# Streaming encoder step on one core: one write for the halves of q and k, and the norms of the cached values moved to the last phase

## The chip, the core and the metric

The kernel runs on one core of one Trainium2 chip. The metric is the device time of one execution in microseconds. The engines are named as in the profile: PE (TensorE), DVE (VectorE), ACT (ScalarE), POOL (GpSimd) and SP (SyncE, whose queue issues nearly all DMAs).

## The reference

One layer with two token mixers. A prompt of 2048 rows and a batch of 8 sample streams with 16 new rows each (128 rows in all) go through the same weights; the samples also attend to 512 cached rows each. The model width is 1024; branch a has 4 heads of differential attention (two 64-wide queries and keys, one 128-wide value), branch b 8 heads of stick-breaking attention (64 wide).

```python
h, gate = adaln_modulate(x, c, norm_g, w_ada, b_ada)
qa, ka, va, za, qb, kb, vb, zb, ga, gb = split(h @ w_in)      # qa, ka are turned by rope
# a: p = softmax(q k^T / 8) for both halves; w = p1 - lam p2; oa = w v   (keys up to the row's chunk of 64)
# b: log_a = log_sigmoid(z) + reversed cumsum of log_sigmoid(-z) over later keys; ob = exp(log_a) v
ya = (rms_norm(oa, subln_g) * (1 - lam_init) * silu(za)) @ w_branch_a
yb = (ob * silu(zb)) @ w_branch_b
x = x + gate * (sigmoid(ga) * ya + sigmoid(gb) * yb) @ w_out
y = rms_norm(x, final_g)
```

The outputs are y for prompt and samples, and the new k and v of both branches. Inputs and outputs are fp32.

## The kernel before

**Numbers.** Large products are made on TensorE from fp16 pairs: a tensor x is scaled by a power of two that is worked out from its norm, and split into a high half (x rounded to fp16) and a low half (the rest). `split` (L316) does it with two instructions: the high half by ScalarE, VectorE or POOL, and the low half by a VectorE `scalar_tensor_tensor` (L324) that reads the source and the high half. A norm is taken with `sum_squares` (L299): one ScalarE activation that squares a tile of 128 x 1024 and adds up each row, the sums go through a small matmul with ones (`total`, L236) and `scales` makes the powers of two on VectorE.

**Tiles and units.** The rows are 17 tiles of 128: t = 0 to 15 the prompt, t = 16 (`NT`) the samples. The heads are 8 units u: an even unit is one head of branch a (`kind` 0, with rope), an odd one two heads of branch b (`kind` 1). For each unit every tile is projected (`project`: 512 columns of q, k, v, z by L468 matmuls into the bank `ps_mm`). Its `finish` copies the bank (`pr`, L482), makes the halves of v, k and q (L319 and L324; q in `query`, L502 and L503, with its own form), and stores new keys and values. In even units POOL and VectorE turn q and k by rope first (`rot`), and the halves are made from `rot`; in odd units they are made out of PSUM (`ps_mm`). `transpose_qk` turns the six 128 x 128 blocks on TensorE into `ps_t`.

**Scores.** `scores` makes a tile's scores with L709 and L710 into the banks `ps_s`. In even units follow exponentials and the row maximum (L603). In odd units ScalarE makes sigmoids (L135, `sc_p` and `ps_s`), VectorE scans (L683) and POOL multiplies (L689). ScalarE casts the weights' high half (L617, `sc_n`) and VectorE takes the low half (L620). A DMA on SP's queue transposes the weights (`wt`), and TensorE multiplies them by v (L766 to L771). The projection of a unit runs beside the scores of the one before it.

**Side work in the unit phase.** A list `spare` of 48 small loads and squares (made in `norms()`, one step of the list loads a 512 KB piece into one of the shared buffers `wa`/`wb` and squares the piece of the step before): 16 for the branch and output weights and 32 for the cached values, 4 for each of 4 heads of both caches (sums in `csums`). `norm_at` (L1044) says at which step (u, t) of the scores the list is drawn from. A second list does the same for the cached keys, which are also cut and written back (`keys_at`).

**Last phase.** After the units, every tile goes through the branch products (L1507), the merge and the output product (L1541), tile after tile. Between these pieces stand the samples' attention to the caches: `sample` gives ten steps a unit (`steps`), and a new unit begins every six (`S_PERIOD`). In it the cached values are loaded (`cache`, steps 3 and 4, L839), split by their scale (`values`, steps 6 and 7, L843: ScalarE high, VectorE low), and multiplied (`output_cached`, L884) by transposed weights `dwt`, which a DMA makes of `dsc`. `finish` joins cached and new parts with factors `dsf`. The scales of all cached values come from `csums` in one piece at the start of this phase (`vs`).

**What sets the order.** The code issues pieces in the order of the step lists, with weights of cost that interleave them (the number beside each piece); the engines' own order is then made by the tile scheduler. Each engine takes its instructions in that order. The DMAs of SP's queue start in order too.

Of the kernel before, what the change touches and what calls it, by code (L numbers as in the profile page):

```python
# [26 lines left out]
P = 128  # L27
# [11 lines left out]
STICK = 14  # L39
# [86 lines left out]
def layer_kernel(ctx: ExitStack, tc: tile.TileContext, a: dict):  # L126
# [14 lines left out]
    def kept(x):  # L141
# [12 lines left out]
        "av": a["cache_a_v"][0].rearrange("b (j p) h e -> p (b j) (h e)", p=P),  # L154
        "bk": a["cache_b_k"][0].rearrange("b (j p) h d -> p (b j) (h d)", p=P),
        "bv": a["cache_b_v"][0].rearrange("b (j p) h d -> p (b j) (h d)", p=P),
# [154 lines left out]
    def add_up_all(acc):  # L311
        col = tiny.tile([P, acc.shape[1]], F32, tag="cols", name="cols", bufs=1)
        V.tensor_reduce(out=col, in_=acc, axis=AX.X, op=ALU.add)
        return col

# [114 lines left out]
    csums = con.tile([P, 8, 4], F32, name="csums")  # L430
    osums = con.tile([P, NT + 1, 4], F32, name="osums")
    qs = c01.enter_context(tc.tile_pool(name="qs", bufs=1))
    qbuf = [qs.tile([P, 2, 2, 2, 64], F16, name=f"qbuf{i}") for i in range(2)]
    for qb in qbuf:
        G.memset(qb[:, 1, :, 1, :], 0.0)
# [11 lines left out]
    def project(U, t):  # L447
# [30 lines left out]
        def finish():  # L478
# [13 lines left out]
            qb = qbuf[t % len(qbuf)]  # L492
            k16 = stg.tile([P, 2, 2, 64], F16, tag="k16", name="k16")
# [6 lines left out]
            def query(src, scale):  # L500
                src = src.rearrange("p (c d) -> p c d", d=64)
                S.activation(out=qb[:, 0, :, :, :], in_=src.unsqueeze(2).to_broadcast([P, 2, 2, 64]), func=AF.Identity, scale=scale)  # L502
                V.scalar_tensor_tensor(out=qb[:, 1, :, 0, :], in0=src, scalar=scale, in1=qb[:, 0, :, 0, :], op0=ALU.mult, op1=ALU.subtract)  # L503
            if kind == 0:
                cosT, sinT = box["r"][:, 0:32], box["r"][:, 32:96]
                x4 = pr[:, 0:256].rearrange("p (c f d) -> p c f d", c=4, f=2)
                rot = stg.tile([P, 256], F32, tag="rot", name="rot")
                r2 = stg.tile([P, 256], F32, tag="r2", name="r2", bufs=1)
                G.tensor_tensor(out=rot.rearrange("p (c f d) -> p c f d", c=4, f=2), in0=x4,
                                in1=cosT.unsqueeze(1).unsqueeze(1).to_broadcast([P, 4, 2, 32]), op=ALU.mult)  # L510
                G.tensor_tensor(out=r2.rearrange("p (c f d) -> p c f d", c=4, f=2), in0=x4[:, :, ::-1, :],
                                in1=sinT.rearrange("p (f d) -> p f d", f=2).unsqueeze(1).to_broadcast([P, 4, 2, 32]),
                                op=ALU.mult)
                G.tensor_tensor(out=rot, in0=rot, in1=r2, op=ALU.add)
# [17 lines left out]
            U["q16", t], U["k16", t] = qb, k16  # L532
# [24 lines left out]
    def transpose_qk(U, t):  # L557
        g, i = t // 4, t % 4
        q16, k16 = U.pop(("q16", t)), U.pop(("k16", t))
        pt = bank("t", F16)  # L560
        for c in range(2):
            T.transpose(pt[:, c * P : (c + 1) * P], k16[:, c, :, :].rearrange("p f d -> p (f d)"), id16)
        for f in range(2):
            for c in range(2):
                j = 2 + f * 2 + c
                T.transpose(pt[:, j * P : (j + 1) * P], q16[:, f, c, :, :].rearrange("p r d -> p (r d)"), id16)
# [243 lines left out]
    def sample(U, dec, qpad, cs, vs, parity):  # L810
# [6 lines left out]
        ik, sv, iv = (x[:, i : i + 1] for i in (cache_column(nk, h),) for x in (cs, vs[:, 0:8], vs[:, 8:16]))  # L817

        def fetch():
# [6 lines left out]
            V.tensor_scalar(out=f[:, 2:4], in0=parity, scalar1=iv, scalar2=ls[:, 1:2] if kind == 0 else 2.0 ** -STICK, op0=ALU.mult, op1=ALU.mult)  # L826
# [78 lines left out]
        for i in range(4):  # L905
            steps[i // 2] += [one(keys, i)]
            steps[3 + i // 2] += [one(cache, i)]
            steps[6 + i // 2] += [one(values, i)]
            steps[7 + i // 2] += [one(output_cached, i)]
        steps[2] += [one(queries)]  # L910
        steps[4] += [one(scores_all)]
        steps[9] += [one(finish)]
        return steps

    def norms():
# [3 lines left out]
        srcs += [(caches[name][:, i * 8 : i * 8 + 8, h * P : (h + 1) * P], csums[:, cache_column(name, h), i : i + 1], 1.0)  # L919
                 for name in ("av", "bv") for h in range(4) for i in range(4)]  # L920
# [3 lines left out]
        def one(k):  # L924
# [4 lines left out]
            if k < len(srcs):  # L929
                src, dst, scale = srcs[k]  # L930
                st = free.pop(0)
                load(out=st if len(src.shape) == 2 else st.rearrange("p (j n) -> p j n", n=P), in_=src)
# [111 lines left out]
    def norm_at(u, t):  # L1044
        return u < 7 and t < NT and (t >= 16 if u == 0 else t >= 9 or u == 6)
# [420 lines left out]
    with ExitStack() as c2:  # L1466
# [7 lines left out]
        vs = scales(total(add_up_all(csums), 8), res, "s_c", 8)  # L1474
# [109 lines left out]
        for u in range(8):  # L1584
            for i, pieces in enumerate(sample(units[u], dec, qpad, cs, vs, parity)):
# [60 lines left out]
```

## Time and profile before

| | |
|---|---|
| runs | 2211.17, 2213.17, 2214.8 us (median 2213.17) |
| profiled execution, its own time | 2222.53 us |
| its span | 2220.8 us, mean granted PE clock 0.98 |
| PE busy | 2050.1 us (92%), weight loads 1092.0 us beside it |
| DVE / ACT / POOL busy | 1746.7 (79%) / 1607.0 (72%) / 716.0 (32%) us |
| SP's DMA queue | 446.96 MB, 82.5% of 16 engines |
| units | scores of unit 0 from 132 us, of unit 7 to 1735 us; last phase from about 1755 us |

The span is what the trace covers; the execution's own time is 1.7 us longer. A row of a group has the busy time, the mean of one instruction in ns, and the idle time of the engine just before them with what ended most of it. A row of waits reads "waiting op and line <- the one it waited for: total us, count, the longest". Idle time of an engine counts only where the end of the program waits for it.

### The profile page before, as it was taken

To read this page: it belongs to the slowest core of one execution; us is meant where nothing else is said; L and a number is where in the kernel's file an instruction comes from. 1 tells how busy PE (TensorE), PEld (TensorE's weight loads), DVE (VectorE), ACT (ScalarE), POOL (GpSimd) and SP (SyncE) were. 2 spreads that over 40 slices of the span, in tenths; PEclk is the share of its full clock that TensorE was granted. 3 is DMA by queue.
4 is the path that set the end of the run, shared out by engine and by line. 5 is a ranking of instruction groups with operands and counts; after the bars stand their busy time and mean duration, and the time that the engine had idled before them with its cause. 6 is when DMAs were issued, how large, how long until landed. Compare 5 with 4: busy or idle time off the path is not lost. (4 is left out here: it accounts for less than half of the span.)

```text
span 2220.8 us, 41264 instructions
## 1 busy us (share of the span) xinstructions
PE 2050.1 (92%) x14504; PEld 1092.0 (49%) x14504; DVE 1746.7 (79%) x3787; ACT 1607.0 (72%) x3216; POOL 716.0 (32%) x620
## 2 busy tenths in 40 slices
PE   3899999999999999999989998999898798999997
PEld 1545555555555455555555554555454344444443
DVE  5668868789887788988778888787689778778863
ACT  3978677788877687978677788876588556666631
POOL 0433024356310444742034356301345322112210
PEclk9999999999999999999999999999999899999999
DMA  9777669799796989979878899985777899999862
GB/s 333 258 246 188 129 149 220 180 220 205 196 261 159 221 197 207 204 198 226 201 194 211 180 229 212 250 182 127 159 160 171 197 264 215 243 240 233 226 147 67
DMA packets 820817, 449.98 MB, mean 203 GB/s; under 512 B 551962, under 2 KB 759114, under 8 KB 820096
## 3 DMA queue, kind: packets, MB, share of 16 engines
q1 hardware_dynamic: 819660, 446.96, 82.5%
q8 instruction: 113, 1.85, 0.3%
q14 instruction: 96, 0.79, 0.1%
q10 hardware_dynamic: 948, 0.39, 0.1%
HBM read 229.87 MB, written 86.02 MB: 142 GB/s over the span
## 5 line engine op out<-in xcount | busy, mean ns | idle before, releaser
L689 POOL TENSOR_TENSOR sc_p<-sc_p,sc_n 128x127 f32<-128x127 f32 (+7 forms) x192 | 311.9, 1628 | 668.7 <-DVE sc_n L683 510.6
L468 PEld LDWEIGHTS <-hs 128*128 128x128 f16 x3120 | 294.0, 99 | 324.4 <-issue 13.7
L468 PE MATMUL ps_mm<-wa,hs 128*128 128x512 f16 x1590 | 393.4, 383 | 8.2 <-DMA hs<-hT_d 6.4
L468 PE MATMUL ps_mm<-wb,hs 128*128 128x512 f16 x1530 | 379.4, 381 | 0.0
L683 DVE TENSOR_TENSOR_SCAN sc_n<-ps_s,sc_n,zero_t 128x512 f32<-128x512 f32 x192 | 245.4, 1278 | 34.4 <-ACT ps_s L135 29.3
L544 PE MATMUL ps_t<-wa,hs 128*128 128x512 f16 x1020 | 244.4, 382 | 3.3 <-DVE qst L577 2.2
L709 PE MATMUL ps_s<-k,qst 128*128 128x512 f16 (+3 forms) x640 | 222.9, 349 | 26.2 <-DVE sc_n L683 21.1
L544 PEld LDWEIGHTS <-hs 128*128 128x128 f16 x1632 | 155.3, 99 | 186.2 <-DVE qst L577 6.2
L620 DVE TENSOR_TENSOR sc_n<-sc_p,sc_n 128x128 f16<-128x128 f32 (+7 forms) x192 | 213.3, 1113 | 37.2 <-ACT sc_n L617 36.6
L135 ACT ACTIVATE sc_p<-ps_s,usc 128x512 f32<-128x512 f32 (+3 forms) x320 | 203.7, 637 | 38.5 <-PE ps_s L710 27.0
L710 PE MATMUL ps_s<-k,qst 128*128 128x512 f16 (+3 forms) x640 | 223.3, 350 | 0.0
L617 ACT CAST sc_n<-sc_p 128x128 f16<-128x128 f32 (+7 forms) x192 | 155.2, 809 | 59.6 <-POOL sc_p L689 58.9
L135 ACT ACTIVATE ps_s<-ps_s,usc 128x512 f32<-128x512 f32 (+3 forms) x320 | 196.0, 612 | 0.0
L544 PE MATMUL ps_t<-wb,hs 128*128 128x512 f16 x612 | 152.1, 383 | 6.7 <-DMA hs<-hT_d 3.3
L1541 PE MATMUL ps_o<-wo,wb 128*128 128x512 f16 x672 | 153.1, 383 | 1.8 <-ACT wb L1315 1.8
L770 PE MATMUL ps_o<-v,wt 128*128 128x128 f16 x1088 | 135.6, 224 | 19.0 <-DMA wt<-sc_n 18.9
L603 DVE TENSOR_SCALAR_CACHE_REDUCE sc_p<-ps_s,usc 128x512 f32<-128x512 f32 (+3 forms) x160 | 106.1, 664 | 30.5 <-PE ps_s L710 18.6
L1546 POOL TENSOR_TENSOR x<-m,x 128x512 f32<-128x512 f32 x32 | 47.1, 1472 | 254.8 <-DVE m L1544 192.3
L771 PE MATMUL ps_o<-v,wt 128*128 128x64 f16 x1088 | 127.3, 196 | 0.0
L683 DVE TENSOR_TENSOR_SCAN sc_n<-ps_s,zero_t 128x128 f32<-128x128 f32 (+3 forms) x128 | 104.1, 814 | 28.1 <-ACT ps_s L135 28.1
L770 PEld LDWEIGHTS <-wt 128*128 128x128 f16 x1088 | 101.4, 100 | 47.4 <-DMA wt<-sc_n 21.7
L1507 PEld LDWEIGHTS <-wa 128*128 128x128 f16 x816 | 77.5, 98 | 92.1 <-issue 6.0
(380 smaller groups left out, 4528.6 us busy)
## 6 DMA issues: line engine op xcount, KB each, us to landing
hs<-hT_d SPq DMA_DIRECT2D x132, 512.0 KB, 5.0
g_d<-gt SPq DMA_DIRECT2D x68, 256.0 KB, 3.4
out_dram<-pr SPq DMA_DIRECT2D x204, 64.0 KB, 3.7
o_d<-o SPq DMA_DIRECT2D x136, 64.0 KB, 2.4
wa<-g_d SPq DMA_DIRECT2D x17, 512.0 KB, 6.8
wb<-g_d SPq DMA_DIRECT2D x17, 512.0 KB, 4.9
hs<-o_d SPq DMA_DIRECT2D x17, 512.0 KB, 4.1
wide<-in_w_ada_dram SPq DMA_DIRECT2D x8, 1024.0 KB, 12.6
```

What stands on the lines that cost most here:

```text
L135: i = S.activation(**kw)
L468: T.matmul(box["p"], box["h"][:, hi, k, :], U["w"][k][:, wi, :], start=(n == 0), stop=(n == 3 * KT - 1))
L544: x = T.matmul(box["g"][:, 0:gw], box["h"][:, hi, k, :], U["wg"][k // per][:, k % per, wi, :], start=(j == 0), stop=(j == 3 * KT - 1))
L617: x = S.copy(out=hi, in_=src)
L620: V.tensor_tensor(out=lo, in0=src, in1=hi, op=ALU.subtract)
L683: V.tensor_tensor_scan(out=dst[:, lo : lo + n][:, ::-1], data0=src[:, 0:n][:, ::-1], data1=zero_t[:, 0:1].to_broadcast([P, n]), initial=fi ...
L689: G.tensor_tensor(out=p[:, 0:m], in0=p[:, 0:m], in1=n[:, 1 : m + 1], op=ALU.mult)
L709: T.matmul(p[:, 0:n], qst[:, c, :], kk[:, c, 0:n], start=True, stop=False)
L710: T.matmul(p[:, 0:n], qst[:, 2 + c, :], kk[:, c, 0:n], start=False, stop=not diag)
L770: T.matmul(po[:, c * P : (c + 1) * P], wt[:, wj, :], vt[:, c, :, :], start=first, stop=False)
L771: T.matmul(po[:, c * P : c * P + 64], wt[:, nb + wj, :], vt[:, c, 0, :], start=False, stop=last)
L1541: T.matmul(po, st["y"][:, yi * 8 + k, :], wo[j * 4 + k // 2][:, wi, k % 2, :], start=(n == 0), stop=(n == 3 * KT - 1))
```

## The change

It has two parts. **Halves:** q and k of a tile get one buffer `qkbuf` of four blocks (q, q, k, k) of 64 columns, each as (high, low, high). One ScalarE instruction writes both high copies of all four blocks (512 elements out, 256 in), and one VectorE instruction the four low halves (256 elements). Before there were two of each: ScalarE 256 and 128 elements, VectorE 128 and 128. The transposed blocks take (high, low) or (low, high) as they lie; what was a zero block beside q's low half is now q's high half there, and the memset of the zeros is gone. That is 136 instructions fewer on ScalarE and 136 on VectorE.

**Cached values:** `norms()` no longer reads them: 32 loads of 512 KB and 32 squares leave the unit phase. `norm_at` draws the list, now 17 pieces long, in units 2, 4 and 6 alone. In the last phase `square` takes the norm of the piece that the sample's own load has brought (steps 4 and 5, one step behind the load), and `value_scale` adds it up at the front of step 6: a reduction, a small matmul into a bank `ps_s`, five small VectorE instructions and the factors in `dsf`. The one piece that made all scales at the phase's start is gone.

```diff
+    qkbuf = [qs.tile([P, 4, 3, 64], F16, name=f"qkbuf{i}") for i in range(2)]
-    for qb in qbuf:
-        G.memset(qb[:, 1, :, 1, :], 0.0)
...
-            def query(src, scale):
-                src = src.rearrange("p (c d) -> p c d", d=64)
-                S.activation(out=qb[:, 0, :, :, :], in_=src.unsqueeze(2).to_broadcast([P, 2, 2, 64]), func=AF.Identity, scale=scale)
-                V.scalar_tensor_tensor(out=qb[:, 1, :, 0, :], in0=src, scalar=scale, in1=qb[:, 0, :, 0, :], op0=ALU.mult, op1=ALU.subtract)
+            def queries_keys(src, scale):
+                src = src.rearrange("p (b d) -> p b d", d=64)
+                S.activation(out=qk[:, :, 0:3:2, :], in_=src.unsqueeze(2).to_broadcast([P, 4, 2, 64]), func=AF.Identity, scale=scale)
+                V.scalar_tensor_tensor(out=qk[:, :, 1, :], in0=src, scalar=scale, in1=qk[:, :, 0, :], op0=ALU.mult, op1=ALU.subtract)
...
-                query(rot[:, 0:128], s)
-                halves(k16, rot[:, 128:256], s)
+                queries_keys(rot, s)
...
-                halves(k16, p[:, 128:256], s2)
-                query(p[:, 0:128], s2)
+                queries_keys(p[:, 0:256], s2)
...
+        for j, (b, r) in enumerate(((2, 0), (3, 0), (0, 0), (1, 0), (0, 1), (1, 1))):
+            T.transpose(pt[:, j * P : (j + 1) * P], qk[:, b, r : r + 2, :].rearrange("p r d -> p (r d)"), id16)
...
+        def square(j):
+            if j == 0:
+                box["acc"] = dec.tile([P, 4], F32, tag="dacc", name="dacc", bufs=2)
+            sum_squares(box["vc", j].rearrange("p b n -> p (b n)"), 1024, box["acc"][:, j : j + 1])
+
+        def value_scale():
+            box["sv"] = x = scales(total(add_up(box.pop("acc"), 4), 1, "s"), dec, "dsv")
+            V.tensor_scalar(out=box["f"][:, 2:4], in0=parity, scalar1=x[:, 1:2], scalar2=ls[:, 1:2] if kind == 0 else 2.0 ** -STICK, op0=ALU.mult, op1=ALU.mult)
...
+            steps[4 + i // 2] += [(0.3, lambda i=i: square(i))]
...
+        steps[6].insert(0, (0.3, value_scale))
...
-        srcs += [(caches[name][:, i * 8 : i * 8 + 8, h * P : (h + 1) * P], csums[:, cache_column(name, h), i : i + 1], 1.0)
-                 for name in ("av", "bv") for h in range(4) for i in range(4)]
...
     def norm_at(u, t):
-        return u < 7 and t < NT and (t >= 16 if u == 0 else t >= 9 or u == 6)
+        return u in (2, 4) and 12 <= t < NT or u == 6 and 9 <= t < NT
...
-        vs = scales(total(add_up_all(csums), 8), res, "s_c", 8)
```

The first place is the end of unit 3 on ScalarE, where the projection of unit 4 has begun beside the last scores of unit 3 (`sc_p` and `ps_s` are sigmoids of those, `csums` a square of cached values). Before:

```order
L617 CAST sc_n<-sc_p 128x1024
L502 ACTIVATE qbuf_213<-rot,sq_11249 128x256
L319 ACTIVATE k_11480<-rot,sq_11249 128x2x64
L482 ACTIVATE pr<-ps_mm,usc_11240 128x512
L319 ACTIVATE v<-ps_mm,usc_11240 128x2x64
L135 ACTIVATE sc_p<-ps_s,usc_8227 128x512
L135 ACTIVATE ps_s<-ps_s,usc_8227 128x512
L299 ACTIVATE junk,csums<-wb_1426 128x1024
L135 ACTIVATE sc_p<-ps_s,usc_8227 128x384
L135 ACTIVATE ps_s<-ps_s,usc_8227 128x384
```

And at the same place after the change (line numbers are those of the changed file, 7 to 16 lower):

```order
L601 CAST sc_n<-sc_p 128x1024
L492 ACTIVATE qkbuf_212<-rot,sq_11006 128x4x2x64
L135 ACTIVATE sc_p<-ps_s,usc_8044 128x512
L135 ACTIVATE ps_s<-ps_s,usc_8044 128x512
L472 ACTIVATE pr<-ps_mm,usc_10997 128x512
L312 ACTIVATE v<-ps_mm,usc_10997 128x2x64
L135 ACTIVATE sc_p<-ps_s,usc_8044 128x384
L135 ACTIVATE ps_s<-ps_s,usc_8044 128x384
```

Two instructions for q and k became one, the square between two pairs of sigmoids is gone, and the first pair stands ahead of the next tile's `pr` and `v`.

The second place is ScalarE in the last phase, at the samples' unit 1 (`dsc` and `ps_t`, `ps_s` are its sigmoids, the cast of `dsc` 128 x 640 is what the DMA to `dwt` waits for; `hs`, `wa`, `wb` belong to the branch products). Before:

```order
L135 ACTIVATE dsc<-ps_s,dsf 128x512
L135 ACTIVATE ps_s<-ps_s,dsf 128x512
L135 ACTIVATE hs_181<-hs_181 128x512
L135 ACTIVATE wa_171<-wa_171 128x1024
L135 ACTIVATE wb_1426<-wb_1426 128x1024
L1315 COPY wa_169<-ps_s 128x1024
L1513 CAST wb_1424<-wa_172 128x512
L617 CAST dsc<-dsc 128x640 x2
```

And after (`dacc` takes the squares of the cached values `dc`):

```order
L135 ACTIVATE dsc<-ps_s,dsf 128x512
L135 ACTIVATE ps_s<-ps_s,dsf 128x512
L297 ACTIVATE junk,dacc<-dc 128x1024
L601 CAST dsc<-dsc 128x640
L297 ACTIVATE junk,dacc<-dc 128x1024
L1505 CAST wb_1400<-wa_176 128x512
L601 CAST dsc<-dsc 128x640
```

A square stands ahead of each of the two casts of the weights.

The third place is VectorE in the last phase, at the samples' unit 0 (`nm` to `dsc` is its softmax, `wa` and `wb` the branch products). Before:

```order
L637 TENSOR_REDUCE nm<-mx 128x2
L1509 SCALAR_TENSOR_TENSOR wa_171<-ps_mm,fuy,wa_171 128x512
L651 RECIPROCAL r<-l 128x2
L652 SCALAR_TENSOR_TENSOR r<-l,r,nlam 128x1
L653 TENSOR_TENSOR r<-r,ls_i 128x1
L658 SCALAR_TENSOR_TENSOR dsc<-dsc,r 128x640
```

And after (`col` is the reduction whose sum the small matmul takes, `sc_q` to `dsv` are the scales):

```order
L306 TENSOR_REDUCE col<-dacc 128x1
...
L642 SCALAR_TENSOR_TENSOR dsc<-dsc,r 128x640
L242 TENSOR_SCALAR sc_q<-ps_s 128x1
L244 TENSOR_SCALAR sc_f<-sc_q 128x1
L246 TENSOR_SCALAR sc_e<-sc_f 128x1
L247 TENSOR_SCALAR sc_e<-sc_f 128x1
L249 TENSOR_SCALAR dsv<-sc_e 128x2
L831 TENSOR_SCALAR dsf<-parity,dsv,ls_i 128x2
```

The sum and its scales, which stood once at the phase's start, now stand in each unit, the reduction ahead of the softmax and the scales behind it.

More of the change, by code (lines that the diff above doesn't have):

```diff
@@ L309, in add_up @@
         return col
[L311 to L314, printed above, removed]
     def split(hi, lo, src, s, on=None):
@@ L429, in layer_kernel @@
     cexp = con.tile([P, 8, 4], I32, name="cexp")
-    csums = con.tile([P, 8, 4], F32, name="csums")
     osums = con.tile([P, NT + 1, 4], F32, name="osums")
     qs = c01.enter_context(tc.tile_pool(name="qs", bufs=1))
-    qbuf = [qs.tile([P, 2, 2, 2, 64], F16, name=f"qbuf{i}") for i in range(2)]
-    for qb in qbuf:
-        G.memset(qb[:, 1, :, 1, :], 0.0)
+    qkbuf = [qs.tile([P, 4, 3, 64], F16, name=f"qkbuf{i}") for i in range(2)]
     silu_z = {}
@@ L490, in finish @@
                 S.activation(out=rings[t % len(rings)], in_=p[:, 384:512], func=AF.Identity, scale=sc[:, 1:2])
-            qb = qbuf[t % len(qbuf)]
-            k16 = stg.tile([P, 2, 2, 64], F16, tag="k16", name="k16")
+            qk = qkbuf[t % len(qkbuf)]
             vt = kvp.tile([P, 2, 2, 64], F16, tag="v", name="v", bufs=V_BUFS)
@@ L531, in finish @@
                 load(out=s_d[U["u"]][:, 6:8, :], in_=vt.rearrange("p c f d -> p c (f d)"))
[L532 removed]
+            U["qk", t] = qk
         g0, gw = GATES[U["u"]]
@@ L558, in transpose_qk @@
         g, i = t // 4, t % 4
-        q16, k16 = U.pop(("q16", t)), U.pop(("k16", t))
+        qk = U.pop(("qk", t))
         pt = bank("t", F16)
[L561 to L566, printed above, removed]
+        for j, (b, r) in enumerate(((2, 0), (3, 0), (0, 0), (1, 0), (0, 1), (1, 1))):
+            T.transpose(pt[:, j * P : (j + 1) * P], qk[:, b, r : r + 2, :].rearrange("p r d -> p (r d)"), id16)
         if t == NT:
@@ L808, in cache_column, with sample @@
         return "ab".index(name[0]) * 4 + h
-    def sample(U, dec, qpad, cs, vs, parity):
+    def sample(U, dec, qpad, cs, parity):
         kind, h, t, sc, sq = U["kind"], U["h"], NT, U["sc"], U["sq"]
@@ L816, in sample @@
         box = {}
-        ik, sv, iv = (x[:, i : i + 1] for i in (cache_column(nk, h),) for x in (cs, vs[:, 0:8], vs[:, 8:16]))
+        ik = cs[:, cache_column(nk, h) : cache_column(nk, h) + 1]
         def fetch():
@@ L931, in one @@
                 st = free.pop(0)
-                load(out=st if len(src.shape) == 2 else st.rearrange("p (j n) -> p j n", n=P), in_=src)
+                load(out=st, in_=src)
                 loaded.append((st, dst, scale))
@@ L1584, in layer_kernel @@
         for u in range(8):
-            for i, pieces in enumerate(sample(units[u], dec, qpad, cs, vs, parity)):
+            for i, pieces in enumerate(sample(units[u], dec, qpad, cs, parity)):
                 if S_PERIOD * u + i == len(lane):
```

4 lines of the change are left out of this document (1 added, 3 removed).

## Prediction, as it was put on record before the changed kernel ran

> **What bounds the kernel now.** I read the page first: its head, its first part (busy time) and its second (forty slices). Under the head line come the first part, and then three rows of slices.
>
> ```profile
> span 2220.8 us, 41264 instructions
> PE 2050.1 (92%) x14504; PEld 1092.0 (49%) x14504; DVE 1746.7 (79%) x3787; ACT 1607.0 (72%) x3216; POOL 716.0 (32%) x620
> PE   3899999999999999999989998999898798999997
> DVE  5668868789887788988778888787689778778863
> ACT  3978677788877687978677788876588556666631
> ```
>
> TensorE is busy for 92% of the span and stands at 9 in most slices, so the time is TensorE's own work plus the 171 us (2220.8 less 2050.1) in which it stands idle. The change leaves the large matmuls as they are. It can therefore only move the idle part, and the question for each edit is which of TensorE's waits it shortens or makes.
>
> Next come three windows at the ends of units 1, 3 and 5 and one over most of the sample lane in the last stretch (the columns are busy time and instruction count of PE, PEld, DVE, ACT and POOL, then clock, DMA share and GB/s).
>
> ```profile
> 480.00:550.00 70.00, 63.86 (x519) 36.42 (x517) 66.20 (x115) 65.43 (x136) 48.21 (x42) 0.98 0.95 203
> 888.00:958.00 70.00, 61.92 (x497) 35.17 (x496) 62.64 (x112) 62.94 (x128) 46.07 (x41) 0.96 0.98 203
> 1300.00:1380.00 80.00, 72.54 (x549) 39.76 (x547) 70.08 (x120) 70.86 (x145) 53.39 (x47) 0.94 1.02 206
> 1850.00:2120.00 270.00, 260.23 (x2063) 127.23 (x2064) 218.82 (x501) 171.61 (x241) 54.46 (x38) 0.99 0.89 230
> ```
>
> At the ends of odd units ScalarE (63 of 70 us) and VectorE (63 to 66 of 70) are nearly full and TensorE loses 6 to 8 us each time. In the last stretch ScalarE is busy 64% and TensorE 96%. So the change takes ScalarE work from places where it is scarce and adds it to a place where it has room, but where TensorE has little slack.
>
> **The part taken away from ends of odd units.** In the waits of TensorE, each of the three windows (480 to 530, 888 to 932, 1300 to 1348) gives the same row, the first below. The other rows are the timeline of ScalarE and VectorE at one of these waits.
>
> ```profile
> PE ps_s L709 <- DVE sc_n L683: 4.1, 3, 1.7
> ...
> 516.88 1.04 ACT L617 CAST sc_n<-sc_p 128x1024 f16<-128x1024 f32 x1
> 517.84 1.05 ACT L299 ACTIVATE junk<-wb 128x1024 f16<-128x1024 f32 x1
> 518.79 0.19 ACT L299 ACTIVATION_READ_ACCUMULATOR junk<-wb 128x1 f32 x1
> 518.89 0.67 ACT L135 ACTIVATE sc_p<-ps_s,usc 128x512 f32<-128x512 f32 x1
> ...
> 519.06 1.21 DVE L683 TENSOR_TENSOR_SCAN sc_n<-ps_s,zero_t 128x512 f32<-128x512 f32 x1
> ...
> 520.32 0.38 PE L709 MATMUL ps_s<-k,qst 128*128 128x512 f16 x1 [1.70 <-DVE sc_n L683]
> ```
>
> A score matmul waits 1.70 us for a bank that a scan frees; ScalarE's sigmoids for that unit stand behind a square, which holds the queue from 517.84 to 518.89, 1.05 us. With the change no norm stands in an odd unit. How many do now is counted by the windows of that line alone at the three ends (here the second column is ScalarE's busy time and count).
>
> ```profile
> 480.00:530.00 50.00, 4.68 (x8) 0.97 0.98 199
> 884.00:932.00 48.00, 3.45 (x6) 0.96 1.01 216
> 1297.00:1348.00 51.00, 3.53 (x7) 0.93 1.05 224
> ```
>
> A square is two records (the activation and the reading of its accumulator), so these are three to four squares and 3.5 to 4.7 us at each end. What else the full engines do there is scans and casts, which stay. The gain is at least one square for each end (3 x 1.05 = 3 us), at most the whole wait (3 x 4.1 = 12.3 us) when the merged halves help too. I take 6 us, two squares an end.
>
> Three windows of 10 us show what such a wait drags behind it: the clock.
>
> ```profile
> 480.00:490.00 10.00, 7.58 (x55) 4.58 (x53) 9.86 (x12) 9.56 (x20) 8.14 (x7) 0.83 0.84 187
> 890.00:900.00 10.00, 7.58 (x54) 4.57 (x53) 9.75 (x13) 9.74 (x20) 8.13 (x8) 0.83 0.86 188
> 1300.00:1310.00 10.00, 7.57 (x54) 4.46 (x53) 7.84 (x13) 8.66 (x17) 8.22 (x8) 0.86 1.27 228
> ```
>
> A granted 0.83 over 10 us is 1.7 us of full clock lost, three times 4.8 us (1.7 + 1.7 + 1.4). If the waits shrink, some of these dips go: bounds 0 and 4.8, I take 2, since a wait must nearly vanish for its dip to go. The Trainium skill ("TensorE: Matmul & The Clock Gate", Part 1) says that the clock is halved after an idle window of about 3.4 us and comes back after a busy one of that length; by that rule waits of 1.7 us would cost no clock and the dips would be no part of the gain. With this term at 0 the sum below would be 4 us in place of 6. The three rows speak against the rule, since the clock falls where TensorE was still busy 7.6 of 10 us.
>
> **The reads taken away.** Thirty-two reads of 512 KB (2 caches x 4 heads x 4) leave the sync queue and the DMA engines. The first and last group of them, two of four, and what even units wait for (600 to 700, 1010 to 1110 and 1370 to 1530 us):
>
> ```profile
> L932 SPq DMA_DIRECT2D wb<-in_cache_a_v_dram x5: 383/412/1706, 826.0 to 1262.9; - x5
> L932 SPq DMA_DIRECT2D wb<-in_cache_b_v_dram x11: 383/384/577, 1278.9 to 1459.1; - x11
> ...
> PE ps_o L766 <- DMA wt<-sc_n: 4.7, 3, 2.7
> ...
> PE ps_o L766 <- DMA wt<-sc_n: 4.2, 3, 2.7
> ...
> PE ps_o L766 <- DMA wt<-sc_n: 5.8, 4, 2.9
> ```
>
> The transposes that TensorE waits for share the sync queue and the DMA engines with these reads. In the first of the three windows no cached value is read, yet 4.7 us are waited, so most of the wait has another source: it cannot fall to nothing. Bounds: 0, and what the second and third window would save if halved together with the first, 7 us. I take 3 us.
>
> **The halves of q and k.** A tile had two ScalarE and two VectorE instructions for q and k, and now has one of each. The groups by form:
>
> ```profile
> L482 ACT ACTIVATE pr<-ps_mm,usc 128x512 f32<-128x512 f32 x68 | 46.9, 690 | 7.4 <-PE ps_mm L468 6.3 <-issue 1.2
> ...
> L502 ACT ACTIVATE qbuf<-rot,sq 128x256 f16<-128x256 f32 x68 | 34.8, 512 | 3.3 <-POOL rot L514 2.9
> L324 DVE SCALAR_TENSOR_TENSOR k<-rot,sq,k 128x128 f16<-128x128 f32 x68 | 32.3, 475 | 0.3 <-ACT k L319 0.3
> L502 ACT ACTIVATE qbuf<-ps_mm,usc 128x256 f16<-128x256 f32 x68 | 32.1, 472 | 44.0 <-DVE k L324 41.6 <-PE ps_t L566 2.3
> L503 DVE SCALAR_TENSOR_TENSOR qbuf<-rot,sq,qbuf 128x128 f16<-128x128 f32 x68 | 32.1, 472 | 6.4 <-ACT qbuf L502 6.3
> L319 ACT ACTIVATE k<-rot,sq 128x128 f16<-128x128 f32 x68 | 27.5, 404 | 10.6 <-PE ps_t L562 10.6
> L319 ACT ACTIVATE k<-ps_mm,usc 128x128 f16<-128x128 f32 x68 | 25.6, 377 | 24.1 <-DVE v L324 23.8
> ```
>
> ScalarE now writes 512 elements, since the key's high half is written twice: priced by the copy of 512 at 690 ns, a tile goes from 512 + 404 = 916 ns to 690 in even units and from 849 to 690 in odd ones, 26 us over 68 of each. On VectorE a tile of an even unit pays 475 + 472 ns; 256 elements in one are priced between one such instruction and 1.5 of it, 0.2 to 0.5 us saved a tile, 15 to 35 us for 68. In odd units ScalarE stood 41.6 us waiting for VectorE's key half before it could write q; that alternation over one PSUM tile is gone. None of this is TensorE's time: projections run tiles ahead of the scores. Its worth is in the full stretches, some five projected tiles for each of the three ends: 5 x 0.23 = 1.1 us on ScalarE each, 3.4 in all for the three. Bounds 0 and, with VectorE's 0.2 us a tile on the path as well (15 x 0.2 = 3), 6; I take 3, nearly all of ScalarE's share, since ScalarE is the engine whose queue the sigmoids stand in.
>
> **What the last stretch gets.** Thirty-two squares, eight sums by a matmul and their scales. Four rows price them, a fifth is the loads' landing time, the last TensorE's wait there (1850 to 2000).
>
> ```profile
> L299 ACT ACTIVATE junk<-wb 128x1024 f16<-128x1024 f32 x64 | 68.0, 1063 | 21.2 <-DMA wb<-in_cache_a_k_dram 11.9 <-DMA wb<-in_cache_b_k_dram 7.6 <-DMA wb<-in_w_in_dram 1.6
> ...
> L308 DVE TENSOR_REDUCE col<-wacc x8: 141/151/158, 19.2 to 1368.3; 128x1 f32<-128x4 f32 x8
> ...
> L236 PEld LDWEIGHTS ps_s<-cacc,ones x64: 186/190/192, 311.5 to 1447.3; 128*128 128x128 f32 x64
> L236 PE MATMUL ps_s<-cacc,ones x64: 167/250/271, 311.8 to 1447.3; 128*128 128x1 f32 x64
> ...
> DMA to landing us min/median/max: 5.6/7.3/9.0
> ...
> PE ps_t L884 <- DMA dwt<-dsc: 9.5, 6, 2.5
> ```
>
> 32 x 1.06 = 34 us of ScalarE, seven of the eight units and so 30 us in the window of 270 us above: from 64% to about 75%. Beside it stand idle gaps, so most is covered. Not covered is what a square delays when it stands ahead of the casts that feed the transposed weights, for which TensorE already waits 9.5 us in six places; unit 1 has two there, 2.1 us. Were that so in all eight units, 17 us; were it nowhere, 0. I take 6 us: three units. The cover, should it go, costs up to 34 us. The sums: two passes of 190 ns of weights each, 8 x 0.38 = 3 us at most on TensorE, VectorE 8 x (0.15 + five small ones of about 0.15) = 7 us beside a VectorE that is 81% busy. TensorE queues its branch and output matmuls behind each sum. I take 2 us, bounds 0 and 6. The loads are in the queue as before, one read of each value less.
>
> **The sum** against the profiled execution, 2222.5 us: -6 (ends) -2 (clock) -3 (transposes) -3 (halves) +6 (squares) +2 (sums) = -6, 2216.5 us. The runs' median is 2213.2, 9.3 us under that execution; the same -6 gives 2207 us, which I take.
>
> **Rivals.** First, slower: the squares wait for their loads at the head of ScalarE's queue. Before, the values' halves came three steps after the loads; a square comes one step after them, and the squares of keys, one step behind their loads too, did wait: the row just shown has 11.9 + 7.6 us ahead of its instructions. For this speaks the landing time of 7.3 us against a step of about 6; against it that a load can be issued once the unit before has freed its buffer, so it may stand earlier than its step. If each of eight units holds ScalarE for 3 us and TensorE gets all of it through the late casts, 24 us come on top of the sum: 2207 + 24 = 2231. It decides from 6 / 8 = 0.75 us a unit on, where the forecast's gain is used up. That the strictly first-in first-out queues of ScalarE and VectorE let everything wait behind one instruction is stated by the Trainium skill ("TensorE: Matmul & The Clock Gate", Part 1), and the timeline at 518 us agrees.
>
> Second, no change: the ends of odd units are set by scans and POOL's products, not by squares. VectorE is as full there as ScalarE (66.2 and 65.4 of 70). Then the ends give 3, clock 0, transposes 2, halves 1, against 6 + 2: +2, 2215 us.
>
> Third, a larger gain: all four gains at their upper bounds, 12.3 + 4.8 + 7 + 6 = 30, with 6 us lost last: -24, 2189 us. For it speaks that ScalarE's 64% leave room for the squares; against it that every upper bound needs VectorE to have time, and it has none at the odd ends.
>
> **The numbers.** Chances: my forecast (gain of 3 to 15 us) 0.46, the third rival 0.15, the second 0.24, the first 0.15. A measurement of this kernel can tell 0.2%, 4.4 us, from no change. The forecast's lower edge lies within that, so of its 0.46 I count 0.36 as faster and 0.10 as same. The second gives 0.18 more to same and, as its +2 may come out past 4.4, 0.06 to slower. Faster 0.36 + 0.15 = 0.51, same 0.28, slower 0.06 + 0.15 = 0.21. The range: 2192 (most of the way to the third) to 2221 (past the second, half way from the forecast to the first); the forecast's own is 2198 to 2210.
>
> **What would show it.** In the profile after: no square in windows 480 to 550, 888 to 958 and 1300 to 1380 and TensorE's wait for the scan there below 4.1 us; the dips at 0.83 fewer; the wait for transposed weights in even units below 4.2 and 5.8; one ScalarE instruction of 512 elements near 0.69 us a tile; in the last stretch ScalarE at 75%, and the wait for the sample's transposed weights above 9.5. I am wrong if that last wait grows by more than 15 us, if squares wait for loads, or if the idle time at the odd ends stays.

## The result: 1.25% slower, and the profile after

The changed kernel takes 2240.4 us (median of 4, 2238.5 to 2247.4) against 2213.7 us: a ratio of 1.0125, 95% interval 1.0107 to 1.0143, so 27 us more where 6 us less was forecast. The later runs were made on several chips, on which the kernel before takes 2212 to 2222 us; so kernels are compared by their ratio to it on their own chip.

The head of the page, the same two rows of slices, and the windows of the prediction, all of the changed kernel:

```profile
span 2238.7 us, 40967 instructions
PE 2056.7 (92%) x14518; PEld 1097.8 (49%) x14518; DVE 1733.3 (77%) x3693; ACT 1599.6 (71%) x3080; POOL 713.5 (32%) x618
PE   3999999998999999999999998999998698999988
ACT  3978677788867677987677788866687567677641
480.00:550.00 70.00, 63.00 (x493) 34.81 (x493) 65.33 (x115) 61.95 (x122) 46.51 (x40) 0.98 0.87 196
888.00:958.00 70.00, 64.56 (x525) 36.28 (x524) 64.99 (x109) 64.45 (x126) 49.97 (x42) 1.00 0.90 187
1300.00:1380.00 80.00, 71.27 (x586) 40.42 (x585) 74.75 (x121) 71.32 (x140) 56.26 (x46) 1.00 0.92 195
1850.00:2120.00 270.00, 251.22 (x1962) 122.17 (x1961) 207.74 (x514) 186.91 (x275) 50.03 (x34) 0.98 0.87 226
```

ScalarE, VectorE and POOL are busy for less time than before, TensorE for 7 us more, and the program takes 27 us longer. In the last window TensorE fell from 260 to 251 us of 270. To cut the time into two stages I take the mask matmuls, which TensorE does once per tile and half in the scores: the first is the start of unit 0, the last the end of unit 7. The rows (minimum, median, maximum in ns, then first and last start) of the kernel before in its second profiled execution, of the halves alone, of the change, and of three of the experiments below (e7, e8, e9):

```profile
L714 PE MATMUL ps_s<-masks,idb x256: 191/217/311, 133.1 to 1731.9; 128*128 128x64 bf16 x64, 128*128 128x128 bf16 x64
L705 PE MATMUL ps_s<-masks,idb x256: 191/218/314, 132.6 to 1726.6; 128*128 128x64 bf16 x64, 128*128 128x128 bf16 x64
L697 PE MATMUL ps_s<-masks,idb x256: 191/205/314, 133.0 to 1734.6; 128*128 128x64 bf16 x64, 128*128 128x128 bf16 x64
L697 PE MATMUL ps_s<-masks,idb x256: 191/217/314, 135.3 to 1725.2; 128*128 128x64 bf16 x64, 128*128 128x128 bf16 x64
L697 PE MATMUL ps_s<-masks,idb x256: 191/217/314, 133.8 to 1720.4; 128*128 128x64 bf16 x64, 128*128 128x128 bf16 x64
L697 PE MATMUL ps_s<-masks,idb x256: 191/217/314, 134.6 to 1718.1; 128*128 128x64 bf16 x64, 128*128 128x128 bf16 x64
```

Unit phase below is last minus first of such a row, last phase the span minus the last. The changed kernel needs 1601.6 + 504.1 us, the one before 1598.8 + 477.4: the units show no gain, and the last phase is 27 us longer. In its first profiled execution, 9 us above the median of its runs, the kernel before had 1602.2 + 486.0; against that one the last phase is 18 us longer. In the table "list" is the list `spare` of the unit phase, and "lane" the row of the samples' steps beside the pieces of the last phase.

| kernel | ratio to before (95%) | unit phase | last phase |
|---|---|---|---|
| before (e0) | 1 | 1598.8 | 477.4 |
| the change; again on another chip (e12) | 1.0125 (1.0107 to 1.0143); 1.0130 (1.0110 to 1.0150) | 1601.6; 1598.9 | 504.1; 504.8 |
| e1 halves alone; again (e13) | 0.9975 (0.9960 to 0.9989); 0.9984 (0.9970 to 0.9999) | 1594.0; 1600.4 | 477.8; 481.2 |
| e2 moved norms alone | 1.0197 (1.0173 to 1.0221) | 1623.6 | 506.3 |
| e3 change, no squares | 1.0119 (1.0098 to 1.0139) | 1601.6 | 499.2 |
| e4 change, squares but no sums | 1.0095 (1.0070 to 1.0120) | 1606.4 | 498.1 |
| e5 change, no squares, no TensorE sum | 1.0042 (1.0023 to 1.0061) | 1605.4 | 494.8 |
| e6 change, norms a step earlier | 1.0144 (1.0120 to 1.0168) | 1601.1 | 508.0 |
| e7 change, list spread as before | 1.0032 (1.0016 to 1.0047) | 1589.9 | 503.6 |
| e8 as e7, lane of before; again (e17) | 0.9935 (0.9919 to 0.9952); 0.9954 (0.9936 to 0.9971) | 1586.6; 1590.1 | 485.8; 485.3 |
| e9 as e8, empty pieces in the lane | 0.9973 (0.9959 to 0.9986) | 1583.5 | 494.1 |
| e10 as e7, cost 0 in the lane | 1.0030 (1.0016 to 1.0044) | 1586.3 | 499.0 |
| e11 as e10, scale at the squares | 1.0026 (1.0014 to 1.0037) | 1584.2 | 503.4 |
| e14 as e10, no squares | 1.0030 (1.0018 to 1.0042) | 1584.2 | 498.7 |
| e15 as e10, no sums | 1.0047 (1.0029 to 1.0066) | 1586.6 | 497.6 |
| e16 halves, reads kept, no squares | 1.0022 (1.0009 to 1.0035) | 1607.9 | 481.3 |

The stages are those of one profiled execution each, the ratios those of all runs. A stage of one and the same kernel differs here by up to 8.6 us between two executions (the last phase of the kernel before; the unit phase of the halves alone by 6.4), so the ratios decide.

### The profile page after: what moved, and what is told of

Its sections match the earlier page's. It is cut to its first block, busy times and chain, and to the rows that moved or that the text cites. A ratio compares the mean times of both kernels' runs of the same rounds, so it can differ in the third digit from the quotient of the medians.

```text
span 2238.7 us, 40967 instructions
## 1 busy us (share of the span) xinstructions
PE 2056.7 (92%) x14518; PEld 1097.8 (49%) x14518; DVE 1733.3 (77%) x3693; ACT 1599.6 (71%) x3080; POOL 713.5 (32%) x618
## 5 line engine op out<-in xcount | busy, mean ns | idle before, releaser
L673 POOL TENSOR_TENSOR sc_p<-sc_p,sc_n 128x127 f32<-128x127 f32 (+7 forms) x192 | 318.5, 1661 | 678.0 <-DVE sc_n L667 520.2
L458 PE MATMUL ps_mm<-wb,hs 128*128 128x512 f16 x1632 | 403.7, 381 | 4.0 <-DVE v L317 4.0
L458 PE MATMUL ps_mm<-wa,hs 128*128 128x512 f16 x1488 | 366.8, 381 | 9.5 <-DVE v L317 9.5
L604 DVE TENSOR_TENSOR sc_n<-sc_p,sc_n 128x128 f16<-128x128 f32 (+7 forms) x192 | 220.0, 1151 | 45.5 <-ACT sc_n L601 45.5
L1533 PE MATMUL ps_o<-wo,wa 128*128 128x512 f16 x672 | 153.3, 383 | 2.8 <-ACT wo L312 2.2
L754 PE MATMUL ps_o<-v,wt 128*128 128x128 f16 x1088 | 131.0, 222 | 16.4 <-DMA wt<-sc_n 15.7
L587 DVE TENSOR_SCALAR_CACHE_REDUCE sc_n<-ps_s,usc 128x512 f32<-128x512 f32 (+3 forms) x160 | 106.2, 664 | 43.4 <-PE ps_s L697 29.0
L755 PE MATMUL ps_o<-v,wt 128*128 128x64 f16 x1088 | 122.8, 195 | 0.0
L499 POOL TENSOR_TENSOR rot<-pr,rope 128x256 f32<-128x256 f32 x68 | 60.3, 886 | 186.3 <-ACT pr L472 157.2
```

Source lines behind the costliest of these rows:

```text
L458: T.matmul(box["p"], box["h"][:, hi, k, :], U["w"][k][:, wi, :], start=(n == 0), stop=(n == 3 * KT - 1))
L587: V.tensor_scalar(out=dst[:, lo : lo + n], in0=p[:, 0:n], scalar1=sc_pos, scalar2=None, op0=ALU.mult, op1=ALU.max, accum_out=job["mx"][:, ...
L604: V.tensor_tensor(out=lo, in0=src, in1=hi, op=ALU.subtract)
L673: G.tensor_tensor(out=p[:, 0:m], in0=p[:, 0:m], in1=n[:, 1 : m + 1], op=ALU.mult)
L754: T.matmul(po[:, c * P : (c + 1) * P], wt[:, wj, :], vt[:, c, :, :], start=first, stop=False)
L1533: T.matmul(po, st["y"][:, yi * 8 + k, :], wo[j * 4 + k // 2][:, wi, k % 2, :], start=(n == 0), stop=(n == 3 * KT - 1))
```

## The experiments

### The two parts apart (e0, e1, e2, e13)

Theory A was that the moved norms make the loss in the last phase; theory B that the new halves cost. e0 is the kernel before; e1 has only the part `qkbuf` / `queries_keys` of the diff, e2 only the rest.

> The kernel before, unchanged, for a second profiled execution: the first one was 9 us above the median of the runs. Both theories expect about 2213 us here, and this trace tells in which phase the 9 us lie: if the scores of unit 7 end near 1726 instead of 1735 us, the changed kernel lost some 9 us in the unit phase; if they end at 1735 again, all 27 us were lost in the last phase.

> The new halves of q and k alone; the cached values are read and normed in the unit phase as before. Theory A (the loss of 27 us is made in the last phase by the moved norms; the halves help a little): 2205 to 2212 us, 1 to 8 us faster than before. Theory B (the halves themselves cost, since the wider ScalarE and VectorE instructions and the new order hold up the unit phase): slower, 2220 us or more.

> The moved norms of the cached values alone, with the halves of before. Theory A: 2240 to 2250 us, the whole loss and what the halves gave back. Theory B: about 2213 to 2222 us.

> The halves alone again, on the chip of the later runs. If the gain does not hang on the chip: 0.996 to 0.999 of before.

Theory B falls: the halves alone gain 5.5 us (0.25% of 2213.7) on one chip and 3.5 us on another. e0 took 2211.1 us with unit 7 ending at 1731.9, where the first execution had 1734.8 and the changed kernel has 1734.6: the loss lies in the last phase. But A is not the whole either: the moved norms alone lose 44 us, 25 of them in the unit phase (1623.6 against 1598.8), from which they take work away. Nor do the two parts add up: the halves are worth 5.5 us alone and 16 us beside the moved norms (1.0197 against 1.0125).

### The last phase: work or order (e3, e4, e5, e6)

```diff
 e3  -            sum_squares(box["vc", j]..., 1024, box["acc"][:, j : j + 1])
     +            V.memset(box["acc"][:, j : j + 1], 1000.0)
 e4  -            box["sv"] = x = scales(total(add_up(box.pop("acc"), 4), 1, "s"), dec, "dsv")
     +            box["sv"] = vs[:, 0:8][:, cache_column(nk, h) : cache_column(nk, h) + 1]
 e5  e3, and
     +            box["sv"] = x = scales(add_up(box.pop("acc"), 4), dec, "dsv")
 e6  cache at steps 2 and 3, square at 3 and 4, value_scale at the front of step 5
```

> The changed kernel without the 32 squares: the sums of squares are set to a constant by a tiny VectorE instruction, so the norms are left out while the small matmuls, the scales in each unit and the order of the pieces stay. Theory A1 (ScalarE's squares in the last phase make the loss): 2205 to 2215 us. Theory A2 (the sums and scales in each unit make it, or the pieces' new order): 2235 us or more. Theory B: 2235 us or more as well.

> The changed kernel with its 32 squares in the last phase kept, but the sums over them and their scales left out: the scales come once, at the start of the phase, from a constant. The last phase took 477 us before and with the halves alone, and 504 us with the change. Theory S (the eight sums with their scales hold up the last phase): it falls back to about 480 us and the time to about 2217 us, since the unit phase keeps its 8 us. Theory O (the order of the pieces, whose costs are unchanged here, holds it up): 500 us and 2235 us or more.

> The changed kernel without squares (constants in their place) and with each unit's sum taken without TensorE: VectorE's reduction is put straight into the scales. What stays is VectorE's chain of eight small instructions in each unit, and the values that wait for it. Theory S1 (the small matmul and the PSUM bank it takes are the cost): last phase about 480 us, time about 2216 us. Theory S2 (the chain of small instructions is the cost, since the values' halves wait for it): last phase near the 499 us of the run without squares, time about 2235 us.

> The changed kernel, complete, with the loads of the cached values, their squares and the scale one step of the lane earlier, and the values' halves where they were. Theory S2 (values late behind their scale): the last phase shortens by 10 us or more, time 2230 us or less. Theory S1 or O: no change within 5 us, about 2240 us.

Without its 32 squares, 34 us of ScalarE, the changed kernel takes the same time (1.0119 against 1.0125). My theory of the queue of squares fell here. Without sums it gains 0.3%, not the 24 us of theory S; without squares and TensorE's sums 0.8%, of which the trace, at the top of its runs, shows 9 us in the last phase. Making the scale ready a step earlier does not help (1.0144), so late scales (S2) are not it. In none of them did the last phase come below 494 us: 17 of the 27 us against e0 stay when the work is gone (9 of 18 against the first execution of the kernel before).

### The unit phase: the steps of the list (e7, e12)

```diff
 e7  +        srcs += [None] * 32          # one(k) does nothing for these
     -        return u in (2, 4) and 12 <= t < NT or u == 6 and 9 <= t < NT
     +        return u < 7 and t < NT and (t >= 16 if u == 0 else t >= 9 or u == 6)
```

> The changed kernel, complete, with the steps of the list of norms as before: the 16 norms of weights stand at the same steps as before, and 32 empty pieces of the same cost stand in the place of the cached values' reads. VectorE's order at the start of unit 2 is then that of the kernel with the halves alone: a v half stands ahead of the burst of eight weight halves. Theory U (the 8 us lost in the unit phase come from the order that the shorter list makes, with a wait of 4 us for a v half in units 2, 4 and 6): the waits go, unit 7's scores end near 1726 us or earlier, and the time is about 2230 us. If the reads' absence itself were the cause: no change, about 2240 us.

> The changed kernel again, beside the next two on one chip, since the chip of the later runs takes some 7 us longer for the kernel before. If the 12 us that the traces show in the unit phase are all that the list's steps cost, it stands at 1.0032 + 12 / 2221 = 1.0086 of before here; if the loss is as on the first chip, at 1.012.

With the list's old steps and 32 empty pieces in it, the same instructions take 0.9% less: 1.0032 against 1.0125 and 1.0130, so e12 lost what the first chip showed and not only the 12 us of the traces. On the chip of e12 the traces give 1598.9 us of unit phase against 1584.2 and 1586.6 of e14 and e15, which have this edit: 12 to 15 us; the medians give some 20. The 5 us or more between them I could not place. The edit does two things, which no run took apart. It puts the 16 loads and squares of the branch and output weights back to their old steps (the loads start between 382 and 812 us in e7, and between 616 and 1456 us in the changed kernel), and it adds the empty pieces. By the code these have cost 0 here (`give` weighs side pieces with 0) and can shift only other side pieces of their own step, so the places of the 16 norms are the likelier cause; that is argued, not shown. What the order does is seen on VectorE at the start of unit 2. In the changed kernel (timeline, two rows of VectorE and two of TensorE; the row of TensorE's waits for 500 to 1560 us; then windows of 4 us, TensorE's busy time after the length, the granted clock third from the end):

```profile
541.21 3.00 DVE L317 SCALAR_TENSOR_TENSOR wa<-wb,sw,wa 128x512 f16<-128x512 f32 x3
544.13 0.34 DVE L317 SCALAR_TENSOR_TENSOR v<-ps_mm,usc,v 128x128 f16<-128x128 f32 x1
...
540.30 0.19 PE L697 MATMUL ps_s<-masks,idb 128*128 128x64 bf16 x1
544.52 2.10 PE L458 MATMUL ps_mm<-wa,hs 128*128 128x512 f16 x6 [4.03 <-DVE v L317]
...
PE ps_mm L458 <- DVE v L317: 12.1, 3, 4.0
...
540.00:544.00 4.00, 0.49 (x10) 0.40 (x8) 4.00 (x5) 3.86 (x9) 2.25 (x3) 1.00 0.71 169
544.00:548.00 4.00, 3.48 (x10) 1.31 (x10) 4.00 (x13) 2.10 (x4) 1.31 (x2) 0.65 1.17 313
...
960.00:964.00 4.00, 0.03 (x2) 0.00 (x0) 4.00 (x7) 3.54 (x9) 2.18 (x2) 1.00 0.86 253
964.00:968.00 4.00, 3.95 (x12) 1.51 (x12) 3.58 (x12) 2.53 (x5) 1.31 (x2) 0.63 1.10 354
```

VectorE makes the low halves of the next unit's weights, eight of them between 535.1 and 544.1 us, and a v half stands behind the last of them. Until it is made, TensorE has no `ps_mm` bank: 4.0 us idle, and then 4 us at 0.65 of the clock, 1.4 us more. Units 2, 4 and 6 each have this wait. In e7 it is gone from unit 2; units 4 and 6 still have 4.0 and 2.7 us. So the expectation that all three go was too much, and these waits are the visible part of the price, not all of it.

### The last phase: pieces without work (e8, e9, e10, e11)

```diff
 e8  e7 with scales once (as e4), and
     -            steps[4 + i // 2] += [(0.3, lambda i=i: square(i))]
     -        steps[6].insert(0, (0.3, value_scale))
 e9  e8 with
     +            steps[4 + i // 2] += [(0.3, lambda: None)]
     +        steps[6].insert(0, (0.3, lambda: None))
 e10 e7 with (0.0, ...) for square and value_scale
 e11 e10 with value_scale at the end of steps[5]
```

> The halves, the list of norms spread over its old steps with empty pieces in the place of the cached values' reads, and in the last phase the samples' lane of before: no squares, no sums and no pieces for them, since the scales come once from a constant (the norms of the cached values are left out altogether). Theory O (the pieces in the lane set another order of the last phase, and that order is most of its 26 us): last phase 477 us, as with the halves alone, and 4 us off the unit phase; about 0.996 of the time before. If instead the last phase is long for what the unit phase leaves behind (other buffers, the state of the queues): last phase 490 us or more.

> The kernel of e8, with empty pieces of the same cost (0.3) in the samples' lane where the squares and the scale would stand. No instruction is added to it; the other pieces of a tile are only interleaved a little differently. Theory O: last phase 490 to 495 us, that is 13 to 18 us longer than e8 with the same instructions. Theory W (the work itself, squares and sums, makes the loss): last phase 477 us, as e8.

> The changed kernel, complete, with the list of norms spread as in e7, and with cost 0 for the squares and the scale in the lane, so that the other pieces stand where they stood before. Theory O: last phase about 487 us (477 and the 10 us that squares and sums cost by e3, e4 and e5), time about 0.999 to 1.000 of before. Theory W: last phase 503 us as in e7, 1.003 of before.

> As e10, but the sum and the scale stand right behind the last squares, at the end of step 5 instead of the front of step 6, so that the values' halves find the scale ready. Theory O: 2 to 5 us less than e10. Theory W: as e10 or 5 us less.

e8 leaves the norms of the cached values out altogether (their scales come from a constant) and takes 0.9935, and 0.9954 on another chip (e17). Its last phase is 485.8 us, 5 to 8 more than with the halves alone; no run explains that, and the first execution of the kernel before had 486.0 too. e9 adds no instruction, only empty pieces, and takes 0.38% more than e8 on the same chip (8 us); against e17 it is 0.19%, with intervals that overlap. Its last phase is 494.1 us, where e8 and e17 have 485.8 and 485.3. The window from 1865 to 2110 us, one row each for the kernel before (e0), e8, e9 and e10:

```profile
1865.00:2110.00 245.00, 239.68 (x1895) 117.56 (x1895) 199.99 (x466) 158.72 (x224) 50.92 (x36) 0.99 0.90 233
1865.00:2110.00 245.00, 234.52 (x1872) 114.50 (x1874) 196.10 (x454) 152.54 (x211) 47.32 (x33) 0.99 0.89 225
1865.00:2110.00 245.00, 228.58 (x1776) 111.12 (x1775) 193.87 (x443) 152.66 (x213) 49.22 (x33) 0.98 0.88 222
1865.00:2110.00 245.00, 227.01 (x1759) 110.98 (x1758) 193.55 (x466) 172.67 (x252) 44.30 (x33) 0.97 0.89 225
```

TensorE loses 5.9 of its 245 us here with the empty pieces alone, and only 1.6 more when ScalarE gets 20 us of squares; e17 has 237.94 in this window, so two executions of one kernel differ by 3.4. What grew from e8 to e9 is the wait for the sample's transposed weights, 9.9 us in e8 (9.3 in e17), and one for a branch product (waits of 1840 to 2130 us in e9):

```profile
PE ps_t L877 <- DMA dwt<-dsc: 13.0, 7, 3.5
PE ps_mm L1504 <- DVE wa L1506: 3.1, 2, 2.1
```

By the medians the real work does add 0.59%, 13.1 us, at the same costs in the lane (e7 against e9), and 12.6 us with cost 0 (e10). Cost 0 does not bring the old order back: e10 and e11 stand where e7 stands, against theory O's 0.999 to 1.000. So the same costs are worth 8 us where the pieces are empty and 0.4 us where they do work (e7 against e10).

### Squares or sums, squares or reads (e14 to e17)

e14 is e10 with the constants of e3, e15 is e10 with the scales of e4; e16 keeps the 32 reads of the halves alone and leaves out the squares behind them.

> The kernel of e10 (list spread, cost 0 in the lane) without the 32 squares (constants by tiny VectorE instructions); the sums and scales of each unit stay. e10 stood at 1.0030 and e9, with neither squares nor sums, at 0.9973. If the squares make those 12 us: 0.998. If the sums make them: 1.002.

> The kernel of e10 with the 32 squares but without sums and scales in each unit (the scales come once from a constant). If the squares make the 12 us: 1.002. If the sums make them: 0.998.

> The halves alone with the 32 reads of cached values kept in the unit phase and their 32 squares left out (the sums come from a constant). The halves alone stood at 0.9975 and 0.9984 of before, e8 (neither reads nor squares) at 0.9935. If ScalarE's squares are what the unit phase gains from: 0.994, as e8. If the reads in the DMA queue are: 0.998, as the halves alone. The forecast's terms were 6 us for the squares and 3 for the reads: 0.995.

> e8 again (the norms of the cached values left out, list of norms and lane as before), beside e16 on one chip. If its place does not hang on the chip: 0.992 to 0.996 of before.

Neither answers as asked. Sums alone cost as much as both (1.0030), squares alone as much or more (1.0047), nothing at all 0.9973: the price does not add up from the pieces of work, so their durations alone do not give it. That it is the order which any added instruction makes is one reading that fits, but it is argued, not shown; two delays that hide each other, one of the squares and one of the sums, would give the same figures, and no run tells the two readings apart. Likewise the squares taken from the unit phase alone give no gain (e16: 1.0022, its unit phase the longest of those with the list spread); only without the reads too does it fall (e17: 0.9954 on the same chip). Whether that is the reads themselves or again an order stays open.

## Why the prediction was wrong

**What failed is a step that it does not contain.** I summed what the change removes and adds and left everything else at its place: of the last stretch I wrote "The loads are in the queue as before", and for the shorter list there is no term at all. But where the pieces of that list and of the samples' lane stand also sets where the others stand. By ratios on the way from e8 to the change (each times 2213.7 us): e8 -14.4, empty pieces in the lane +8.4 (e9), the work in it +13.1 (e7 against e9), and the list's new steps +20.6 (the change against e7) make +27.7, the time measured. So the term put at nothing is the list's new steps, 20.6 us, and the lane, put at +8 for squares and sums, came to 21.5. The gains, forecast at -14, are -14.4 in e8 (-10.2 in e17), but that is luck in part: the terms below do not bear it out one by one. The path through these runs is one of several. With the work put in first, the work is 21.0 us (e10 against e8) and its cost in the lane 0.4 (e7 against e10), and e14 and e15 show that the terms do not simply add. So the 8.4 us hang on the path; and beyond the three waits of 4 us, why the list's new steps cost 20.6 us stays open.

**Ends of odd units (-6).** The prediction's windows (480 to 530, 884 to 932 and 1297 to 1348 us) hold 7.00, 5.93 and 7.10 us of squares with the halves alone; in the changed kernel the first holds 4.57 us, four norms of the next unit's weights (the loads just before them are of `in_w_in`), the other two none. The waits for scans in them, of the changed kernel and then of the halves alone:

```profile
PE ps_s L693 <- DVE sc_n L667: 1.4, 2, 0.8
PE ps_s L693 <- DVE sc_n L667: 3.8, 4, 1.5
...
PE ps_s L701 <- DVE sc_n L675: 1.1, 2, 0.5
PE ps_s L701 <- DVE sc_n L675: 2.9, 3, 1.5
PE ps_s L701 <- DVE sc_n L675: 0.2, 1, 0.2
```

12.3 us became 9.0 (the second row stands for two windows). The halves alone, with the squares in place, have 4.2 in this execution and 9.0 in another (e13). So the cause that I named from one timeline, the square at 517.84, was wrong. In the kernel before, the last sigmoid that can have fed the scan of 519.06 ended at 516.87, ahead of the square; from 514.94 on VectorE was busy without a gap with halves of q, k and v and then with a low half of the attention weights (517.65), and the scan came behind these. In e13 the same square stands at 516.12, but VectorE reaches the scan at 515.60, and TensorE's wait of 1.70 us is 0.50. The rows of the kernel before, then of e13:

```profile
516.17 0.70 ACT L135 ACTIVATE ps_s<-ps_s,usc 128x512 f32<-128x512 f32 x1
517.65 1.49 DVE L620 TENSOR_TENSOR sc_n<-sc_p,sc_n 128x1024 f16<-128x1024 f32 x1
...
515.60 1.21 DVE L675 TENSOR_TENSOR_SCAN sc_n<-ps_s,zero_t 128x512 f32<-128x512 f32 x1
516.86 0.38 PE L701 MATMUL ps_s<-k,qst 128*128 128x512 f16 x1 [0.50 <-DVE sc_n L675]
```

Taking the squares away shortened this wait no further (two of 0.57 and 0.81 us in the changed kernel). TensorE's idle time in the prediction's three windows was 21.7 us before and is 21.2 now: it stayed, which I had named as a sign of being wrong.

**Clock (-2).** The three dips at 0.83 and 0.86 are gone; these are the same windows:

```profile
480.00:490.00 10.00, 10.00 (x74) 5.39 (x74) 9.76 (x13) 10.00 (x20) 8.60 (x7) 1.00 0.95 233
890.00:900.00 10.00, 7.54 (x61) 4.22 (x60) 7.74 (x12) 7.66 (x14) 8.36 (x8) 1.00 0.86 203
1300.00:1310.00 10.00, 10.00 (x70) 5.35 (x69) 7.66 (x12) 6.18 (x13) 6.49 (x5) 1.00 1.05 268
```

Three others came, behind the new waits of 4 us shown above. The gain was right where I looked and was in part taken back 50 to 80 us later. It can't be put down to the moved norms: of the halves alone one execution has no dip in these windows either (e1), another has two at 0.83 (e13).

**Transposed weights (-3).** In the windows of the prediction 4.7 + 4.2 + 5.8 us became 1.0 + 4.4 + 0.5:

```profile
PE ps_o L750 <- DMA wt<-sc_n: 1.0, 1, 1.0
...
PE ps_o L750 <- DMA wt<-sc_n: 4.4, 5, 1.9
...
PE ps_o L750 <- DMA wt<-sc_n: 0.5, 1, 0.5
```

That is 8.8 us less, above my upper bound. But the second execution of the kernel before (e0) has only 9.5 us in these windows, the halves alone, with all reads in place, 8.6 and 9.2 (e1, e13), and the changed kernel 7.3 in its second execution (e12). So most of the 8.8 is not the reads' doing; against the halves alone 1.3 to 3.3 us are left, which fits the 3 that I took but is less than two executions of one kernel differ by.

**Halves (-3).** Right: -5.5 and -3.5 us. Their rows:

```profile
L492 ACT ACTIVATE qkbuf<-rot,sq 128x512 f16<-128x512 f32 x68 | 50.4, 741 | 26.2 <-POOL rot L504 25.9
L492 ACT ACTIVATE qkbuf<-ps_mm,usc 128x512 f16<-128x512 f32 x68 | 47.8, 704 | 21.7 <-DVE v L317 20.5 <-PE ps_t L550 1.1
L493 DVE SCALAR_TENSOR_TENSOR qkbuf<-rot,sq,qkbuf 128x256 f16<-128x256 f32 x68 | 46.1, 678 | 5.7 <-ACT qkbuf L492 5.4
```

741 and 704 ns for 690 priced; VectorE's 678 ns lies within 475 to 712.

**Squares and sums (+6, +2).** ScalarE came to 186.9 of 270 us, 69% where I had 75%. The first rival's mechanism, squares that wait for their loads, is not it:

```profile
L297 ACT ACTIVATE junk<-dc 128x1024 f16<-128x1024 f32 x32 | 33.8, 1056 | 4.1 <-DMA dc<-in_cache_a_v_dram 3.5
```

3.5 us in all, not 3 a unit. Its 2231 us came nearer than my forecast by accident. Nor did the wait for the sample's transposed weights grow, as I had said would show me wrong. The waits of 1840 to 2130 us, first of e0, then of the changed kernel:

```profile
PE ps_t L885 <- DMA dwt<-dsc: 6.6, 7, 2.4
PE ps_t L854 <- DVE o L898: 1.0, 1, 1.0
PE ps_t L885 <- ACT v16c L320: 0.2, 1, 0.2
...
PE ps_t L877 <- DMA dwt<-dsc: 7.4, 8, 2.3
PE ps_s L854 <- ACT wa L1308: 3.4, 1, 3.4
PE ps_s L1307 <- DVE dsc L667: 2.4, 2, 1.4
PE ps_mm L1499 <- DVE wa L1501: 2.2, 2, 1.9
PE ps_t L877 <- DVE v16c L317: 1.5, 3, 0.7
PE ps_t L877 <- ACT v16c L312: 1.5, 2, 0.9
PE ps_s L234 <- DVE col L306: 1.4, 1, 1.4
```

What was 7.8 us in three rows became 19.8 in these seven (21.2 with two smaller rows). Of the seven, 4.4 us are for the halves of the cached values and their sum (`v16c`, `col`); 8.0 are for other engines' steps of the branch products and scans. A changed order fits that better than one slow step, but that too is argued.

## What to carry to other kernels

Where pieces are interleaved by cost and a scheduler makes the engines' order, a piece taken out moves all the others: price the new order as a term with a sign of its own, wide (here 4 to 8 us for empty pieces in the lane and some 20 us for the list's steps, with no instruction added), and don't read "less work" as "not slower". To measure it, put an empty piece of the same cost where the work was, as e9 did, and put what stays back to its old places, as e7 did: that made the same instructions some 20 us faster. Do the two in separate runs, which these did not, and run a kernel more than once before reading a stage of it. Of this change the halves are the part to keep: they alone beat both kernels (0.9975, 0.9984).

## What the runs showed of the chip that I had not expected

A wait of 4.0 us costs more than itself: TensorE's clock stays at 1.00 while it waits, and stands at 0.65 and 0.63 for the next 4 us, when it has work again. The Trainium skill ("TensorE: Matmul & The Clock Gate", Part 1) puts the halving behind an idle window of about 3.4 us, and by that a wait of 4.0 us had to bring a dip; the prediction used the rows of the old dips against it, where two short waits fell together. There the kernel before shows TensorE busy 2.14 of 4 us and then 0.57 of the clock:

```profile
480.00:484.00 4.00, 2.14 (x21) 1.28 (x19) 3.86 (x4) 3.89 (x8) 3.23 (x3) 1.00 0.90 195
484.00:488.00 4.00, 3.44 (x25) 2.36 (x25) 4.00 (x8) 4.00 (x9) 2.99 (x3) 0.57 0.80 171
```

So a window need not be idle throughout. The two waits, 1.47 and 0.95 us, lie between 481.51 and 484.56 us with 0.63 us of matmuls between them, and the clock stands at 0.50 from 485 to 487 us. How much of a window may be busy, no run here tells.
